# A hybrid decoder layer in split float32: 128-row score matmuls throughout, and FFN inputs that stream hi and lo of x side by side

## The chip, the core and the metric

The kernel runs on one core of a Trainium2 chip. TensorE (PE) multiplies matrices into PSUM, VectorE (DVE), ScalarE (ACT) and GpSimd (POOL) work on rows of 128 partitions, and SyncE (SP) issues most DMA transfers. The metric is the device time of one execution in microseconds, and less is better.

## What is computed

The layer works on 256 tokens of width 1024 in float32. Every sub-layer ends in x ← LayerNorm(2^0.25·x + sub-layer(x)).

```python
def swiglu_ffn(x, w_in, w_out):                       # 1024 -> 2 x 2816 -> 1024
    gate, up = jnp.split(x @ w_in, 2, axis=-1)
    return (jax.nn.silu(gate) * up) @ w_out

def dsa block(ql, qi, wi, t):                         # 128 queries, 16 heads
    logits = relu(einsum('bqhd,bsd->bqhs', qi, k_idx))          # index scores, d = 64
    score = where(causal, einsum('bqhs,bqh->bqs', logits, wi), -inf)
    _, idx = lax.top_k(score, 64)
    s = einsum('bqhr,bqkr->bqhk', ql, c_kv[idx]) - slopes * (t - idx)
    return softmax(where(idx <= t, s, -inf)) @ c_kv[idx]

x = LN(ALPHA * x + 0.5 * swiglu_ffn(x, ffn1))
h = x @ w_in                                          # gates, z, xbc, dt, q, c_kv, q_idx, k_idx, w_idx
y_ssd, y_att = ssd_branch(...), dsa_branch(...)       # Mamba-2 scan beside sparse attention
x = LN(ALPHA * x + (sigmoid(g_ssd) * (y_ssd @ w1) + sigmoid(g_att) * (y_att @ w2)) @ w_out)
x = LN(ALPHA * x + memory_xattn(x, mem))              # 4 heads of 256, 256 memory rows
x = LN(ALPHA * x + 0.5 * swiglu_ffn(x, ffn2))
```

## The kernel before

**Split products.** A float32 operand a is kept as two float32r tensors, hi (a rounded, made by an ACT copy) and lo = a − hi (a DVE subtraction); `split` makes both. A product takes three matmuls into one bank, hi·hi, hi·lo and lo·hi (`mm3`), and `mm` issues each. Tokens by features are kept transposed, as pairs of tiles `x0Th` and `x0Tl` ([128 features, 8 K blocks, 256 tokens]; `pairT` makes such a pair, x0T to x3T for the input and behind each norm).

**Weights** arrive by DMA in pieces of 128x1024 (`raw`, four buffers), and each is split at once into `whi` and `wlo` (six buffers of each, so three units of two pieces).

**FFN inputs.** `ffn_in` runs over 22 blocks of 128 features. One of them, a unit, needs a gate block and an up block, each 8 K blocks deep. `a_unit` puts both into one bank ([gate | up], 256 columns each) with 48 matmuls of 256 columns; then silu of the gate (ACT, L321), the product with up (DVE, L322) and a split into the features `ah` and `al`, which are the operands of the FFN's output (matmuls of 512 columns). In FFN 1 the first two units run K block by K block while weights and tokens arrive (`first_units`), in four banks; in FFN 2 the first three units run token block by token block (`by_token`) in another form.

**Mixers.** Three streams of work, sparse attention (`dsa`), the scan (`ssd`) and other projections (`fill_mixers`), are merged by `fly` into one order by a count of matmul work. A score group (`scores`, one head) is four matmuls: for each token block one with the queries' tile over all 128 partitions, and one over 64 partitions:

```python
self.mm(o, q[:, hh // 2, ts], kh, True, False)
self.mm(o, q[r, hh // 2, ts], kl[r], False, True)
```

The queries' tile `w2a` (even heads) or `w2e` (odd heads) holds hi on one half of the partitions and lo on the other (`project`); the keys `kh` hold hi on both halves, so one matmul over 128 rows gives hi·hi + lo·hi. The second one takes the half `r` with the queries' hi, and the keys' lo, for hi·lo. The index keys are `kidxh` and `kidxl`, those of the attention lie in a tile `kv` that `keys_values` makes four heads at a time (L763 to L766, with the values' hi and lo behind them in the same tile). The index scores are weighted and added up in `acc` on DVE, 64 keys are chosen there, and the attention's softmax runs on DVE and ACT.

**Banks and queues.** PSUM has four buffers `mm`, two `s` (scores) and two `t` (transposes). Each engine runs its instructions in the order that a scheduler has fixed.

Of the kernel before, what the change touches and what calls it, by code (L numbers as in the profile page):

```python
"""Hybrid decoder layer (macaron SwiGLU, Mamba-2 SSD beside DSA attention, memory
cross-attention, SwiGLU; DeepNorm post-LayerNorms) on one core.

float32 products go through the tensor engine as three float32r passes: every
operand a is split on the chip into hi (a rounded to float32r) and lo = a - hi,
and a.b = hi.hi + hi.lo + lo.hi accumulates in PSUM.  Small products stay float32.
"""
# [18 lines left out]
P = 128  # L26
# [24 lines left out]
class Layer:  # L51
# [28 lines left out]

    def tap(self, name, tile_):
        if name in self.taps:
            self.nc.sync.dma_start(self.taps[name], tile_)

# [4 lines left out]
    def weight(self, ap, piece=1024, pool=False):  # L89
        """loads, split into (hi, lo) in pieces of columns; pool: GpSimd makes the last lo."""  # L90
# [26 lines left out]
    def fly(self, *streams):  # L117
        """emits several streams of work in one order: a stream yields after a piece either
        how long (us of matmul work) its next piece should wait for the other engines, or the
        name of a result that another stream marks as done."""  # L120
# [17 lines left out]
    def mm3(self, out, a, b, start, stop):  # L138
        """out (+)= a^T b; a, b = (hi, lo)."""
        self.mm(out, a[0], b[0], start, False)  # L140
        self.mm(out, a[0], b[1], False, False)
        self.mm(out, a[1], b[0], False, stop)
# [5 lines left out]
    def a_block(self, ps, w, xT):  # L148
        """w: (hi, lo) [p, 128] per K block, stationary; ps [128 features, 256 tokens]."""
        for k, wk in enumerate(w):  # L150
            self.mm3(ps, wk, (xT[0][:, k, :], xT[1][:, k, :]), k == 0, k == len(w) - 1)

    def a_unit(self, ap, xT):
        """two 128-column blocks, [p, (2, kb, 128)], by 256 tokens in one bank."""
# [11 lines left out]
    def b_part(self, ps, w, xT, tb, k, start, stop):  # L166
        """tokens of block tb stationary, one K block w (hi, lo) [p, n] moving."""
# [11 lines left out]
    def b_chunk(self, wap, xT, evac, width=512):  # L179
        """[2, p, (4 kb, width)] columns, both token blocks in turn."""  # L180
# [32 lines left out]
    def constants(self):  # L213
# [7 lines left out]
        # attention keys: [0:256] for the queries of block 1, [256:384] for block 0  # L221
# [27 lines left out]
    def ln_params(self, i):  # L249
        """(scale, shift) of layer norm i, each as two halves of the columns."""  # L250
# [14 lines left out]
    def layer_norm(self, r, st, gb, dst):  # L265
        """r [128, 1024] with bn statistics st; dst may be r."""
# [11 lines left out]
    def res_evac(self, ps, c, r, x, scale, st):  # L278
        """r = scale * ps + x in the columns from c, with their statistics."""
# [11 lines left out]
    def ffn_in(self, win, xT, slots, first=None, by_token=0):  # L291
        """silu(gate) * up as hi/lo by features; the first by_token units run one token block
        after the other, so that the matmuls need not wait for the second."""
# [18 lines left out]
        for j in range(by_token, NFF):  # L312
            if first and j < 2:
                gate, up = first[2 * j:2 * j + 2]
            else:
                ps = self.a_unit(win[j], xT)
                gate, up = ps[:, :T], ps[:, T:]
            sg = self.small([P, T], "wa", bufs=4)
            if late:
                self.act_T(*late.pop())  # L320
            nc.scalar.activation(sg, gate, AF.Silu)  # L321
            nc.vector.tensor_mul(sg, up, sg)  # L322
# [6 lines left out]
    def first_units(self, xT):  # L329
        """tokens and the first two units of FFN 1 K block by K block, as they arrive; the  # L330
        tensor engine and the activation tables are warmed up meanwhile."""
# [9 lines left out]
        ps = [self.psum("mm")[:, :T] for _ in range(4)]  # L341
        for q in range(4):
# [10 lines left out]
            for k in range(2 * q, 2 * q + 2):  # L353
                for i in range(4):
                    c = slice((k % 2) * 512 + i * P, (k % 2) * 512 + (i + 1) * P)
                    self.mm3(ps[i], (hi[:, c], lo[:, c]), (xT[0][:, k, :], xT[1][:, k, :]), k == 0, k == KB - 1)
# [7 lines left out]
    def ffn_out(self, wout, act, finish, skew=3, last=False):  # L364
        """last: the columns that end last are finished in two parts."""
# [684 lines left out]
```

## Time and profile before

| | |
|---|---|
| Time of three runs | 835.6, 834.26, 835.91 us |
| Median | 835.6 us |
| Profiled execution, span | 833.3 us (no other time is recorded of it) |
| PE busy | 816.3 us, 98% of the span, 5726 matmuls |
| DVE, ACT, POOL busy | 560.8 us (67%), 424.1 us (51%), 68.1 us (8%) |
| Chain that ended last | PE 89%, DVE 4%, issue 4%, DMA 1%, ACT 1% |

The span runs from the first to the last instruction that the profile shows. An engine's busy share is an average over stages that differ. The granted clock is a fraction of TensorE's full speed: 1.00 is 2.4 GHz, 0.50 is 1.2 GHz. A timeline's line gives start, duration, engine, line, operation, tiles and count; durations of matmuls overlap, so what a matmul takes of PE's time is read from the starts. The stages lie as follows: FFN 1's input to about 135 us, its output to 195, the mixers to about 500, the cross-attention to about 635, FFN 2's input from there to 767 and its output to the end.

### The profile page before, as it was taken

The page shows a single profiled execution, that of the slowest core. Times are in us where ns is not written, and L with a number is a line of the kernel's source. Part 1 is how long each engine was busy: PE and PEld are TensorE (multiplying, and loading weights), DVE is VectorE, ACT ScalarE, POOL GpSimd, SP SyncE. Part 2 cuts the span into 40 slices and gives each one's busy share as a digit, 9 for nine tenths or more (in the row PEclk, how much of TensorE's full clock was granted, in tenths as well). Part 3 has the DMA queues.
Part 4 walks back from the last instruction along what each step waited for, and adds up shares of the span by engine and source line. Part 5 has one row for each costly group of instructions (what it writes and reads, how often), then busy time and mean ns, then how long its engine had stood idle before and what let it go on. Part 6 is the DMA issues. An engine that isn't in the chain of part 4 may idle for free.

```text
span 833.3 us, 14320 instructions
## 1 busy us (share of the span) xinstructions
PE 816.3 (98%) x5726; PEld 758.1 (91%) x5726; DVE 560.8 (67%) x870; ACT 424.1 (51%) x700; POOL 68.1 (8%) x69
## 2 busy tenths in 40 slices
PE   8999999999989899999999999999999999999996
PEld 7999999887889887899999998889988999999885
DVE  5665555449598988598778767965659755555445
ACT  5564444324666584477566545454444644444430
POOL 1100000000024351130000000100001000000000
PEclk9999999999999998999999999999999999999998
DMA  7886555554556513226444355685434755555531
GB/s 246 275 281 212 178 181 184 194 176 130 193 191 240 180 49 107 72 77 217 150 126 153 117 174 182 199 271 172 151 119 134 260 184 179 187 190 179 185 120 51
DMA packets 39923, 142.97 MB, mean 172 GB/s; under 512 B 4592, under 2 KB 4896, under 8 KB 39472
## 3 DMA queue, kind: packets, MB, share of 16 engines
q1 hardware_dynamic: 38016, 134.63, 49.0%
q0 software_dynamic: 1840, 7.43, 2.9%
q8 instruction: 45, 0.74, 0.4%
q14 instruction: 22, 0.18, 0.1%
HBM read 140.97 MB, written 1.06 MB: 170 GB/s over the span
## 4 chain that ended last, share of the span: by engine, by line
PE 89%; DVE 4%; issue 4%; DMA 1%; ACT 1%; POOL 0%; SPq 0%; DVEq 0%; ACTq 0%; POOLq 0%
PE ps_mm L111 79%; PE ps_s L111 5%; DVE wlo L146 2%; PE ps_t L115 2%; PE ps_t L111 2%; DMA raw<-in_ffn_in_dram 1%; DVE wa L430 1%; ACT whi L145 0%; DVE spp L503 0%; DVE bcT L430 0%; POOL rstd L262 0%; DVE bst L285 0%; ACT L432 0%; SPq L349 0%; DVE x L282 0%
## 5 line engine op out<-in xcount | busy, mean ns | idle before, releaser
L146 DVE TENSOR_TENSOR wlo<-raw,whi 128x1024 fp32r<-128x1024 f32 (+2 forms) x245 | 302.2, 1236 | 184.8 <-ACT whi L145 183.3
L145 ACT CAST whi<-raw 128x1024 fp32r<-128x1024 f32 (+2 forms) x253 | 262.4, 1041 | 222.1 <-PE ps_mm L111 111.5
L111 PE MATMUL ps_mm<-x1Th,whi 128*128 128x256 f32 x384 | 112.4, 293 | 0.0
L111 PE MATMUL ps_mm<-x1Tl,whi 128*128 128x256 f32 x384 | 110.9, 289 | 0.0
L111 PE MATMUL ps_mm<-x1Th,wlo 128*128 128x256 f32 x384 | 110.8, 289 | 0.0
L111 PE MATMUL ps_mm<-x0Th,whi 128*128 128x256 f32 x352 | 99.7, 285 | 1.4 <-ACT whi L145 1.3
L111 PE MATMUL ps_mm<-x0Tl,whi 128*128 128x256 f32 x352 | 99.2, 283 | 0.0
L111 PE MATMUL ps_mm<-x0Th,wlo 128*128 128x256 f32 x352 | 98.3, 284 | 0.7 <-DVE wlo L146 0.7
L111 PE MATMUL ps_mm<-x3Th,whi 128*128 128x256 f32 x304 | 86.2, 284 | 0.0
L111 PE MATMUL ps_mm<-x3Th,wlo 128*128 128x256 f32 x304 | 86.0, 283 | 0.0
L111 PE MATMUL ps_mm<-x3Tl,whi 128*128 128x256 f32 x304 | 86.0, 283 | 0.0
L111 PEld LDWEIGHTS ps_mm<-x1Th,whi 128*128 128x128 f32 x384 | 75.5, 197 | 1.3
L111 PEld LDWEIGHTS ps_mm<-x1Tl,whi 128*128 128x128 f32 x384 | 75.5, 197 | 0.4 <-issue 0.4
L111 PEld LDWEIGHTS ps_mm<-x1Th,wlo 128*128 128x128 f32 x384 | 75.7, 197 | 0.1
L111 PEld LDWEIGHTS ps_mm<-x0Th,whi 128*128 128x128 f32 x352 | 67.7, 192 | 2.5 <-ACT whi L145 2.5
L111 PEld LDWEIGHTS ps_mm<-x0Th,wlo 128*128 128x128 f32 x352 | 66.9, 192 | 1.3 <-DVE wlo L146 1.3
L111 PEld LDWEIGHTS ps_mm<-x0Tl,whi 128*128 128x128 f32 x352 | 67.7, 192 | 0.0
L111 PE MATMUL ps_mm<-whi,ah 128*128 128x512 f32 x154 | 60.4, 392 | 0.0
L111 PE MATMUL ps_mm<-wlo,ah 128*128 128x512 f32 x154 | 60.1, 390 | 0.0
L111 PE MATMUL ps_mm<-whi,al 128*128 128x512 f32 x154 | 59.9, 389 | 0.0
L111 PEld LDWEIGHTS ps_mm<-x3Tl,whi 128*128 128x128 f32 x304 | 58.4, 192 | 0.0
L111 PEld LDWEIGHTS ps_mm<-x3Th,wlo 128*128 128x128 f32 x304 | 58.4, 192 | 0.0
(305 smaller groups left out, 1708.9 us busy)
## 6 DMA issues: line engine op xcount, KB each, us to landing
raw<-in_ffn_in_dram SPq DMA_DIRECT2D x87, 512.0 KB, 4.4
raw<-in_ffn_out_dram SPq DMA_DIRECT2D x44, 512.0 KB, 4.4
raw<-in_w_xbc_dram SPq DMA_DIRECT2D x16, 512.0 KB, 4.3
raw<-in_w_gate_dram SPq DMA_DIRECT2D x16, 512.0 KB, 3.6
raw<-in_w_z_dram SPq DMA_DIRECT2D x8, 512.0 KB, 4.4
raw<-in_w_qidx_dram SPq DMA_DIRECT2D x8, 512.0 KB, 4.1
raw<-in_w_q_dram SPq DMA_DIRECT2D x8, 512.0 KB, 3.7
raw<-in_w_pssd_dram SPq DMA_DIRECT2D x8, 512.0 KB, 4.1
```

The lines of the kernel that those rows point to most:

```text
L111: self.nc.tensor.matmul(out, a, b, start=start, stop=stop)
L115: self.nc.tensor.transpose(out, in_, self.ident)
L145: self.nc.scalar.copy(hi, src)
L146: (engine or self.nc.vector).tensor_sub(lo, src, hi.bitcast(F32))
L430: self.last_conv = nc.vector.scalar_tensor_tensor(v[:, d:], src[:, :T - d], cw[:, 3 - d:4 - d], v[:, d:], op0=ALU.mult, op1=ALU.add)
```

## The change

In the FFN inputs hi and lo of x lie in one tile (`wideT`, [128, 2, 8, 256]). `pair` does a K block with two matmuls instead of three: the weights' hi past both halves (512 columns, into [hi·hi | hi·lo] of a whole bank) and the weights' lo past x hi (256 columns, onto the first half). `pair_unit` takes a bank for the gate and one for up. `join` adds the two halves: an ACT copy of the second into SBUF, and a DVE addition of the first. In `scores` the second matmul runs over 128 rows too, so that the lo halves of the queries meet the keys' lo as well; for this `keys_values` writes the keys' lo on both halves of the partitions (one more DVE subtraction per i, two per call, four calls), and the values' hi and lo move to a small tile of their own (`w2c`). Comments and docstrings are gone from the new file, which moves line numbers.

```diff
+    def wideT(self, name):
+        v = self.bp.tile([P, 2, KB, T], F32R, tag="g12", name=self.nm(name))
+        return v[:, 0], v[:, 1], v
+    def pair(self, ps, w, x, k):
+        self.mm(ps, w[0], x[2][:, :, k, :], k == 0, False)
+        self.mm(ps[:, :T], w[1], x[0][:, k, :], False, k == KB - 1)
+    def pair_unit(self, ap, xT):
+        out = []
+        for w in self.weight(ap):
+            ps = self.psum("mm")
+            for k in range(KB):
+                self.pair(ps, tuple(v[:, k * P:(k + 1) * P] for v in w), xT, k)
+            out.append(ps)
+        return out
+    def join(self, ps, out):
+        self.nc.scalar.copy(out, ps[:, T:])
+        self.nc.vector.tensor_add(out, out, ps[:, :T])
+        return out
...
-                ps = self.a_unit(win[j], xT)
-                gate, up = ps[:, :T], ps[:, T:]
-            sg = self.small([P, T], "wa", bufs=4)
+                gate, up = self.pair_unit(win[j], xT)
+            sg, u = self.small([P, T], "wa", bufs=4), self.small([P, T], "wa", bufs=4)
             if late:
                 self.act_T(*late.pop())
-            nc.scalar.activation(sg, gate, AF.Silu)
-            nc.vector.tensor_mul(sg, up, sg)
+            nc.scalar.activation(sg, self.join(gate, sg), AF.Silu)
+            nc.vector.tensor_mul(sg, self.join(up, u), sg)
...
-        ps = [self.psum("mm")[:, :T] for _ in range(4)]
+        ps = [self.psum("mm") for _ in range(4)]
...
-                    self.mm3(ps[i], (hi[:, c], lo[:, c]), (xT[0][:, k, :], xT[1][:, k, :]), k == 0, k == KB - 1)
+                    self.pair(ps[i], (hi[:, c], lo[:, c]), xT, k)
...
-            r, q = slice((hh % 2) * HD, (hh % 2 + 1) * HD), q[hh % 2]
+            q = q[hh % 2]
...
-                self.mm(o, q[r, hh // 2, ts], kl[r], False, True)
+                self.mm(o, q[:, hh // 2, ts], kl, False, True)
...
-        kl = s[:, 1024:1536].rearrange("p (a b) -> p a b", b=T)
-        vh, vl = s[:, 1536:1792], s[:, 1792:]
+        kl = s[:, 1024:].rearrange("p (i a b) -> p i a b", i=2, b=T)
+        v0 = self.small([P, 2, T], "w2c", F32R, 2)
+        vh, vl = v0[:, 0, :], v0[:, 1, :]
...
             nc.scalar.copy(kh[a, i], ps[a])
-            nc.vector.tensor_sub(kl[a], ps[a], kh[a, i].bitcast(F32))
             nc.scalar.copy(kh[b, i], ps[a])
+            nc.vector.tensor_sub(kl[a, i], ps[a], kh[a, i].bitcast(F32))
+            nc.vector.tensor_sub(kl[b, i], ps[a], kh[a, i].bitcast(F32))
...
-        xT = self.pairT(1, 2, "x0T")
+        xT = self.wideT("x0T")
```

(The last replacement stands four times, for x0T to x3T.)

**One unit of FFN 1 on PE.** Before, from the last K block of the gate into the first of up; each group of three stands eight times for each half, and the bank `ps_mm_806` is the same for both:

```order
L111 MATMUL ps_mm_806<-x0Th_72,whi_808 128x256
L111 MATMUL ps_mm_806<-x0Tl_73,whi_808 128x256
L111 MATMUL ps_mm_806<-x0Th_72,wlo_809 128x256
L111 MATMUL ps_mm_806<-x0Th_72,whi_814 128x256
L111 MATMUL ps_mm_806<-x0Tl_73,whi_814 128x256
L111 MATMUL ps_mm_806<-x0Th_72,wlo_815 128x256
```

After, the last K block of the gate, the first of up in another bank, and the first of the next unit in a third; each group of two stands eight times for each bank:

```order
L116 MATMUL ps_mm_715<-x0T_72,whi_704 128x512
L116 MATMUL ps_mm_715<-x0T_72,wlo_705 128x256
L116 MATMUL ps_mm_732<-x0T_72,whi_710 128x512
L116 MATMUL ps_mm_732<-x0T_72,wlo_711 128x256
...
L116 MATMUL ps_mm_771<-x0T_72,whi_760 128x512
L116 MATMUL ps_mm_771<-x0T_72,wlo_761 128x256
```

The 48 instructions of a unit have become 32, and a unit holds two banks instead of one.

**The same unit on DVE.** Before, the product of gate and up (`wa_867`), the features' lo (`al`), two subtractions for weights of a later unit, and the next unit's product:

```order
L322 TENSOR_TENSOR wa_867<-ps_mm_806,wa_867 128x256
L146 TENSOR_TENSOR al_264<-wa_867,ah_261 128x256
L146 TENSOR_TENSOR wlo_1073<-raw_1071,whi_1072 128x1024
L146 TENSOR_TENSOR wlo_1079<-raw_1077,whi_1078 128x1024
L322 TENSOR_TENSOR wa_933<-ps_mm_872,wa_933 128x256
```

After, the two additions of `join`, the product, a weight's lo, the features' lo and a weight's lo:

```order
L177 TENSOR_TENSOR wa_749<-wa_749,ps_mm_715 128x256
L177 TENSOR_TENSOR wa_750<-wa_750,ps_mm_732 128x256
L348 TENSOR_TENSOR wa_749<-wa_750,wa_749 128x256
L151 TENSOR_TENSOR wlo_879<-raw_877,whi_878 128x1024
L151 TENSOR_TENSOR al_231<-wa_749,ah_228 128x256
L151 TENSOR_TENSOR wlo_929<-raw_927,whi_928 128x1024
```

Two additions out of the banks now stand ahead of the product, which reads SBUF only.

**The end of the first two units on DVE.** Before, the last weights' lo of these units and of unit 2, and the two products, `wa_266` and `wa_271`:

```order
L146 TENSOR_TENSOR wlo_199<-raw_196,whi_198 128x1024
L146 TENSOR_TENSOR wlo_279<-raw_277,whi_278 128x1024
L146 TENSOR_TENSOR wlo_285<-raw_283,whi_284 128x1024
L322 TENSOR_TENSOR wa_266<-ps_mm_85,wa_266 128x256
L322 TENSOR_TENSOR wa_271<-ps_mm_87,wa_271 128x256
L146 TENSOR_TENSOR wlo_345<-raw_343,whi_344 128x1024
```

After, in the same place (`ps_mm_83` to `ps_mm_86` are the four banks of the two units):

```order
L151 TENSOR_TENSOR wlo_174<-raw_171,whi_173 128x1024
L151 TENSOR_TENSOR wlo_255<-raw_253,whi_254 128x1024
L151 TENSOR_TENSOR wlo_261<-raw_259,whi_260 128x1024
L177 TENSOR_TENSOR wa_233<-wa_233,ps_mm_83 128x256
L177 TENSOR_TENSOR wa_234<-wa_234,ps_mm_84 128x256
L177 TENSOR_TENSOR wa_243<-wa_243,ps_mm_85 128x256
L177 TENSOR_TENSOR wa_244<-wa_244,ps_mm_86 128x256
L348 TENSOR_TENSOR wa_233<-wa_234,wa_233 128x256
L151 TENSOR_TENSOR wlo_311<-raw_309,whi_310 128x1024
```

The same three subtractions come first; then the four additions, where only the two products stood.

**One call of keys_values on DVE.** Before, the keys' lo (L765, 64x512), the accumulation of index scores (`acc`) and the values' lo (L146) between the two subtractions:

```order
L765 TENSOR_TENSOR kv_3204<-ps_mm_3206,kv_3204 64x512
L669 SCALAR_TENSOR_TENSOR acc_3015<-wa_3230,widx_2227,acc_3015 128x256
L669 SCALAR_TENSOR_TENSOR acc_3015<-wa_3230,widx_2227,acc_3015 128x128
L146 TENSOR_TENSOR kv_3204<-ps_mm_3234,kv_3204 128x256
L669 SCALAR_TENSOR_TENSOR acc_3015<-wa_3255,widx_2227,acc_3015 128x256
L669 SCALAR_TENSOR_TENSOR acc_3015<-wa_3255,widx_2227,acc_3015 128x128
L765 TENSOR_TENSOR kv_3204<-ps_mm_3206,kv_3204 64x512
```

After, the keys' lo is written twice per i (L793 and L794), and the values' lo goes into `w2c`:

```order
L793 TENSOR_TENSOR kv_2980<-ps_mm_2983,kv_2980 64x512
L794 TENSOR_TENSOR kv_2980<-ps_mm_2983,kv_2980 64x512
L695 SCALAR_TENSOR_TENSOR acc_2791<-wa_3009,widx_2003,acc_2791 128x256
L695 SCALAR_TENSOR_TENSOR acc_2791<-wa_3009,widx_2003,acc_2791 128x128
L151 TENSOR_TENSOR w2c_2981<-ps_mm_3013,w2c_2981 128x256
L695 SCALAR_TENSOR_TENSOR acc_2791<-wa_3034,widx_2003,acc_2791 128x256
L695 SCALAR_TENSOR_TENSOR acc_2791<-wa_3034,widx_2003,acc_2791 128x128
L793 TENSOR_TENSOR kv_2980<-ps_mm_2983,kv_2980 64x512
L794 TENSOR_TENSOR kv_2980<-ps_mm_2983,kv_2980 64x512
```

The order around them is as it was. On PE the score groups stand where they stood, between the same neighbours.

## Rows read from the trace of the kernel before

**Rows 1.** The page: busy time by engine; granted clock in 40 slices, in tenths.
```profile
PE 816.3 (98%) x5726; PEld 758.1 (91%) x5726; DVE 560.8 (67%) x870; ACT 424.1 (51%) x700; POOL 68.1 (8%) x69
...
PEclk9999999999999998999999999999999999999998
```

**Rows 2.** The page: shares of the span of the chain that ended last, by line.
```profile
PE ps_mm L111 79%; PE ps_s L111 5%; DVE wlo L146 2%; PE ps_t L115 2%; PE ps_t L111 2%; DMA raw<-in_ffn_in_dram 1%; DVE wa L430 1%; ACT whi L145 0%; DVE spp L503 0%; DVE bcT L430 0%; POOL rstd L262 0%; DVE bst L285 0%; ACT L432 0%; SPq L349 0%; DVE x L282 0%
```

**Rows 3.** Windows of the FFNs: PE, PEld, DVE, ACT, POOL, clock, DMA share, GB/s.
```profile
60.00:130.00 70.00, 70.00 (x586) 70.00 (x585) 39.95 (x50) 33.13 (x50) 0.00 (x0) 1.00 0.58 193
690.00:755.00 65.00, 65.00 (x544) 65.00 (x543) 35.49 (x45) 30.81 (x46) 0.00 (x0) 1.00 0.54 181
```

**Rows 4.** Window of FFN 1's output, PE alone.
```profile
142.00:190.00 48.00, 48.00 (x214) 1.00 0.54 175
```

**Rows 5.** The chain of work in order of time, in FFN 2's output.
```profile
767.38 0.71 PE ps_t L111 x6
768.09 2.07 PE ps_mm L111 x9
```

**Rows 6.** Groups of instructions by line, form and tile.
```profile
L146 DVE TENSOR_TENSOR wlo<-raw,whi 128x1024 fp32r<-128x1024 f32 x239 | 297.3, 1246 | 181.2 <-ACT whi L145 179.7 <-PE ps_mm L111 0.5
...
L145 ACT CAST whi<-raw 128x1024 fp32r<-128x1024 f32 x247 | 258.1, 1049 | 218.9 <-PE ps_mm L111 111.2 <-issue 61.6 <-PE ps_t L111 24.2
...
L322 DVE TENSOR_TENSOR wa<-ps_mm,wa 128x256 f32<-128x256 f32 x41 | 17.0, 417 | 0.0
...
L321 ACT ACTIVATE wa<-ps_mm 128x256 f32<-128x256 f32 x41 | 15.6, 380 | 0.4 <-PE ps_mm L111 0.3
...
L765 DVE TENSOR_TENSOR kv<-ps_mm,kv 64x512 fp32r<-64x512 f32 x8 | 5.5, 688 | 0.4 <-ACT kv L764 0.2
```

**Rows 7.** Timelines of DVE and of PE at the end of the first two units.
```profile
16.90 3.73 DVE L146 TENSOR_TENSOR wlo<-raw,whi 128x1024 fp32r<-128x1024 f32 x3 [1.88 <-ACT whi L145]
...
18.18 0.62 PE L111 MATMUL ps_mm<-x0Th,wlo 128*128 128x256 f32 x3 [0.16 <-DVE wlo L146]
```

**Rows 8.** Timeline of PE at the first group of index scores.
```profile
297.46 0.28 PE L111 MATMUL ps_s<-kidxh,w2a 128*128 128x256 f32 x1
297.67 0.38 PE L111 MATMUL ps_s<-kidxl,w2a 64*128 64x256 f32 x1
297.98 0.38 PE L111 MATMUL ps_s<-kidxh,w2a 128*128 128x256 f32 x1
298.29 0.38 PE L111 MATMUL ps_s<-kidxl,w2a 64*128 64x256 f32 x1
298.61 0.66 PE L115 MATMUL ps_t<-ident,bcT 128*128 128x128 f32 x4
```

**Rows 9.** Timeline of PE at a group of attention scores.
```profile
423.72 1.30 PE L111 MATMUL ps_s<-kv,w2a 128*128 128x256 f32 x4
424.94 0.39 PE L111 MATMUL ps_mm<-yTh,whi 128*128 128x256 f32 x1
425.16 0.28 PE L111 MATMUL ps_mm<-yTl,whi 128*128 128x256 f32 x1
```

**Rows 10.** The chain of work at scores of the cross-attention.
```profile
571.80 1.42 PE ps_s L111 x12
```

**Rows 11.** Windows of index scores and top-k, and of the attention.
```profile
297.00:366.00 69.00, 69.00 (x435) 59.33 (x434) 55.32 (x119) 39.06 (x75) 18.43 (x10) 0.93 0.22 70
366.00:476.00 110.00, 110.00 (x824) 101.82 (x824) 88.57 (x190) 73.09 (x179) 5.58 (x5) 1.00 0.45 144
```

**Rows 12.** Windows of 1 us at two falls of the clock.
```profile
316.00:317.00 1.00, 1.00 (x4) 0.61 (x3) 0.97 (x2) 0.27 (x1) 0.00 (x0) 0.73 0.87 344
317.00:318.00 1.00, 1.00 (x3) 0.55 (x3) 0.97 (x4) 0.49 (x1) 0.00 (x0) 0.50 0.11 29
...
347.00:348.00 1.00, 1.00 (x3) 0.50 (x2) 1.00 (x3) 0.37 (x1) 0.98 (x1) 0.59 0.00 0
348.00:349.00 1.00, 1.00 (x5) 0.97 (x5) 0.93 (x1) 0.53 (x3) 0.44 (x1) 0.50 0.00 0
```

More of the change, by code (lines that the diff above doesn't have):

```diff
@@ L689, in softmax_in @@
             kv = self.kv[u]
-            ps = scores(qs[u], hh, kv[0][:, hh % 2, hh // 2, :], kv[1][:, hh // 2, :])
+            ps = scores(qs[u], hh, kv[0][:, hh % 2, hh // 2, :], kv[1][:, hh % 2, hh // 2, :])
             p = p_[h] = self.small([P, 384], "wa", bufs=4)
@@ L902, in run @@
             self.scale_res(x, tb)
-        xT = self.pairT(1, 2, "x1T")
+        xT = self.wideT("x1T")
         def fin(gb, dst, n=2):
@@ L943, in run @@
         gb = self.ln_params(2)
-        xT = self.pairT(1, 2, "x2T")
+        xT = self.wideT("x2T")
         self.proj_ln(t["w_out"], mT, x, gb, next_T(xT))
@@ L973, in run @@
         gb = self.ln_params(3)
-        xT = self.pairT(1, 2, "x3T")
+        xT = self.wideT("x3T")
         self.proj_ln(t["w_mo"], oT, x, gb, next_T(xT), (probs, turn, values))
```

## The prediction

> **What bounds the kernel now.** I read the page first: TensorE (PE) is busy 816.3 of 833.3 us and the chain that ended last runs over it for 89% of the span, 79% of that on the products into the mm banks, 5% on score matmuls [rows 1, 2]. So a shorter PE instruction stream shortens the kernel, as long as VectorE (DVE, 67% busy) and ScalarE (ACT, 51%) can follow. Shares over the whole span don't answer that, so each stage that the change touches is read by itself below.
>
> The profiled span is 833.3 us; the three runs have a median of 835.6, and I put the 2.3 us between them around the span, unchanged. Sums are made on the span, and a difference in the span is carried to the time. About 0.2%, 1.7 us, is what a measurement here can tell from no change.
>
> **FFN inputs.** For each 128-column block and K block there were three matmuls of 256 columns; now there is one of 512 and one of 256, the same 768 columns in two instructions. By the code, 39 units (20 in FFN 1, 19 in FFN 2) hold 16 such pairs, 624 pairs; the 32 pairs of the first two units wait for weights and are left out. In two stretches inside the FFNs PE has no idle time; 70.00 us hold 584 whole matmuls (586 less two cut at the edges) and 65.00 hold 542 [rows 3]: 0.1199 us for 256 columns, 5.76 us per unit of 48. In the FFN output, where all are 512 wide, 48.00 us hold 212: 0.2264 us [rows 4]. A pair would then save 3×0.1199−0.2264−0.1199 = 0.0134 us, 624 of them 8.4 us: the upper bound. The lower bound is from the one place where both widths take turns, FFN 2's output: six of 256 columns take 0.71 us and nine of 512 take 2.07, together 2.78 [rows 5], where 6×0.1199+9×0.2264 is 2.757. If the missing 0.023 us is the price of going from one width to the other and back, every pair pays it and loses 0.0096 us: 6.0 us more. The row can't say whether the surplus comes with each change of width or otherwise (the six also go to other banks than the nine), so I take most of the upper bound: **−5.6 us**, with −8.4 to +6.0 kept.
>
> The Trainium skill speaks against this part: "TensorE: Matmul & The Clock Gate", section "Back-to-back issue gap", has a fixed surplus of about 2.5 ns per matmul over its columns, by which 624 fewer instructions would save 1.6 us. Our two rows differ by 0.1065 us for 256 columns, so each matmul carries 0.0134 us beyond its columns here; the measured rows decide, and the sum goes by them.
>
> **Joins.** Each unit adds two ACT copies and two DVE additions of 128x256. Their nearest rows are the silu out of a bank, 380 ns, and the multiplication out of a bank, 417 ns [rows 6]. In the stretches of [rows 3] a unit (5.76 us) has 39.95/12.2 = 3.3 us of DVE and 33.13/12.2 = 2.7 us of ACT, so 4.1 and 3.5 after, below the 5.54 us that PE will need (16×0.3463). Following the order by hand (cast, copy, silu, copy, cast on ACT; weights' lo, two additions, multiplication, lo on DVE), with casts of 1049 and subtractions of 1246 ns [rows 6], the next unit's first addition comes about 7 us after this unit's gate bank ends, and that is inside the two units that four banks give. On ACT the copy of the up bank waits for PE's last matmul of the unit, and two casts of weights stand behind it; these are for a unit well ahead, so nobody waits for them yet. **0 us**, hidden behind PE; without that cover it is the last rival below. That hi and lo of x now share a tile, and that values' hi and lo moved, adds no instruction: 0.
>
> **The start.** Here a wait is new. All four banks are taken by the first two units, and unit 2's first matmul gets the first bank only after the DVE addition, which stands behind three weight subtractions. These start at 16.90 and end at 20.63 [rows 7]; before, the bank was free after a silu on ACT. PE ended the first two units near 20.2: the three lo matmuls from 18.18 on are followed by 14 more, (3+14)×0.12 after it [rows 7]. With the addition the bank is free at 20.63+0.42 = 21.05: **+0.9 us** (0 if subtractions come sooner, 1.7 if both additions must pass). Behind this wait on PE stands all of unit 2.
>
> **Score matmuls.** There are 32 groups (16 index heads, 16 attention heads), each of four matmuls of 256 columns: over 128 rows, 64, 128, 64. Starts in an index group are 297.46, .67, .98, 298.29, and the next instruction comes at 298.61 [rows 8]: 0.21+0.31+0.31+0.32 = 1.15 us, and a matmul behind a group takes 0.22 until the next instead of 0.12 (the first one behind the attention group: 424.94 to 425.16 [rows 9]). Together 1.25 where four at full pace take 0.48: **0.77 saved**. The attention group runs from 423.72 to 425.16, the matmul after it included: 1.44−5×0.12 = 0.84. That 128 rows are the cure is shown by the cross-attention's scores, same shapes over 128 rows: twelve in 1.42 us, 0.118 each [rows 10]. The lowest count, only what lies inside a group (1.15−0.48 = 0.67), gives 21.4 us, the highest (0.84) 26.9. I take **−24.6 us**. What it costs: keys' lo on both partition halves, 8 more DVE subtractions of 64x512 at 688 ns [rows 6], counted below.
>
> **Clock.** The granted clock is 1.00 almost everywhere [rows 1], but 0.93 in 297 to 366 [rows 11]. In 1 us slices it falls from 316 and from 347 on and is 0.50 (1.2 GHz) a microsecond later; 4 and 3 matmuls begin in the microsecond of the fall, as in the score groups, where at full pace there are 8 [rows 12]. 69.00×0.07 = 4.8 us is lost there. If those pauses go, it should mostly come back; new waits could bring it down again. **−4.0 us** (0 to −4.8).
>
> **DVE in the mixers: the price of all this.** From 297 to 366 DVE is busy 55.32 us of 69.00, from 366 to 476 88.57 of 110.00 [rows 11]; PE has no idle time there, so PE sets the pace. After the change PE needs 69.00−16×0.77−4.0 = 52.7 and 110.00−12.3 = 97.7; DVE, with four of the added subtractions in each (0.69 apiece), 58.1 and 91.3. In the first stretch DVE is then the longer by 5.4 us, and in the second it has 6% left. The order on PE hardly changes, so PE, and all that stands behind on it, waits for what DVE is late with: converted queries, the accumulation of index scores ahead of top-k, weights' lo. Lower bound 0 (DVE's lag is absorbed by weights three units ahead and made up before 500), upper bound: DVE keeps half of its idle time of the first stretch (13.7/2) on top of 5.4, 12.3. I take the 5.4 and some of the second stretch: **+7 us**.
>
> **Sum.** −5.6+0.9−24.6−4.0+7 = −26.3: span 807.0, time **809.3 us**.
>
> **Rivals.**
> *DVE takes over in the mixers.* It loses 13 to 19 instead of 7, because its operations wait for ACT and PE in turn. For it: its work comes to 110% and 93% of PE's in the two stretches, and two engines that wait for each other at such shares seldom reach the longer one's sum. Against: weights can be prepared ahead, and most of the second stretch's 6% is free. 815 to 821.
> *DVE hides it all.* −8.4+0.5−24.6−4.8 = −37.3: 798.3. For it: weights are prepared three units ahead; against: top-k runs on DVE between index scores and attention, and nothing is ahead of it.
> *The widths cost.* What a pair saves goes with the turn from 512 to 256 columns and back. With half of the surplus of [rows 5] a pair keeps 0.0134−0.0115 = 0.0019 us, 1.2 in all: 813.7. With all of it the FFN loses 6.0: 820.9. For it: that row; against: it shows the surplus once in fifteen matmuls, along with a change of banks. "TensorE: Matmul & The Clock Gate" of the Trainium skill, by its gap alone, would put the time at 813.3.
> *The pauses are not from the 64 rows* but from the alternation of banks or operands; then scores gain nothing, DVE is no bound and the clock stays: −5.6+0.9: 830.9. Against it stands [rows 10].
> *Slower.* ACT and DVE wait for each other in each FFN unit (copy, silu, addition, multiplication, cast, lo are one chain over two in-order engines), and this cycle becomes the pace of 39 units. Strictly in turn they need 4.1+3.5 = 7.6 us. All other terms give −20.7, so it decides from (20.7+1.7)/39 = 0.57 us above 5.76, at 6.3 us per unit; at 7.6 the FFNs lose 72 and the time is 887. Against it: the casts and subtractions of weights, 4.6 us of the 7.6, depend on DMA alone.
>
> **Chances.** Forecast (DVE term 0 to 12, FFN gaining) 0.47; DVE takes over 0.20; all hidden 0.14; widths cost 0.10; pauses stay 0.05; slower 0.04. The range 798 to 822 holds the first four cases, with a little of their edges outside, and leaves out the last two. The first five are all faster by over 1.7 us; 0.02 is kept for a mixture that ends near no change: faster 0.94, within 0.2% 0.02, slower 0.04.
>
> **What would show it.** Score groups with starts 0.12 us apart; units of 32 matmuls in 5.54 us inside the FFNs without idle time on PE (5.9 if widths cost, over 6.3 if the joins bound); a granted clock of 1.00 from 297 on; a PE wait of near 0.9 us for the first addition at about 20; and in the mixers PE waits for DVE of some 7 us in sum, most ahead of the attention. The forecast is wrong if those waits pass 20 us, or if PE waits for a join anywhere but at the start.

## The result and the profile after

The changed kernel takes 815.08 us in the median of four runs (813.47 to 816.25), beside 835.75 for the kernel before on the same chip: a ratio of 0.9757, 95% interval 0.9735 to 0.9778. It is faster by 2.4%. The forecast was 809.3, in a range of 798 to 822.

The page of the changed kernel, span 812.9 us: busy time by engine, the granted clock in tenths, and the two lines of the chain that ended last.

```profile
PE 789.4 (97%) x5070; PEld 717.5 (88%) x5070; DVE 592.4 (73%) x960; ACT 448.4 (55%) x782; POOL 68.2 (8%) x69
...
PEclk9999999999999999799999999999999999999999
...
PE 74%; DVE 11%; issue 8%; ACT 4%; DMA 2%; POOL 1%; SPq 0%; DVEq 0%; ACTq 0%; POOLq 0%
PE ps_mm L116 69%; DVE wlo L151 3%; PE ps_t L116 2%; PE ps_t L120 2%; DMA raw<-in_ffn_in_dram 2%; ACT whi L150 1%; PE ps_s L116 1%; DVE acc L695 1%; DVE acc L702 1%; DVE wa L456 1%; DVE m L701 1%; DMA raw<-in_w_pssd_dram 0%; POOL rstd L289 0%; DVE kv L794 0%; DVE kv L793 0%
```

PE is still busy 97% of a span that is 20.4 us shorter, but its share of the chain has fallen from 89% to 74% and DVE's has risen to 11% [rows 1, 2]. One slice of the clock now shows 7. It lies where the index scores are. By the first starts of the matmuls on each tile, the 20.4 us come from these stretches:

| stretch (from the end of the one above) | before | after | difference |
|---|---|---|---|
| to FFN 1's output | 135.5 | 134.3 | −1.2 |
| to the first index scores | 162.0 | 159.7 | −2.3 |
| to the first attention scores | 69.4 | 64.8 | −4.6 |
| to the projection of the attention's output | 118.8 | 110.5 | −8.3 |
| to FFN 2's output | 281.5 | 277.5 | −4.0 |
| to the end | 66.1 | 66.1 | 0.0 |

Nothing of the change runs in the second stretch; over all kernels of this study it takes 159.7 to 164.1 us. PE's pauses in its last 70 us sum to 4.4 to 6.7 us, and in all but three of the kernels the clock falls there. A difference of 2 us between two profiles is therefore not read as an effect here.

What PE waits for in the changed kernel up to 500 us, the eight largest (sum, times, longest):

```profile
PE ps_t L120 <- DVE cTl L501: 3.1, 1, 3.1
PE ps_s L116 <- ACT wa L692: 2.6, 1, 2.6
PE ps_mm L116 <- ACT whi L150: 2.1, 4, 1.0
PE ps_t L116 <- DVE warm L362: 1.3, 1, 1.3
PE ps_s L116 <- DVE w2a L668: 1.2, 1, 1.2
PE ps_mm L116 <- ACT S0xe L613: 1.0, 1, 1.0
PE ps_mm L116 <- DVE wa L177: 0.9, 1, 0.9
PE ps_t L120 <- DVE yTl L231: 0.9, 1, 0.9
```

New among them are the wait for the join at the start (`wa` L177, 0.9) and four in the mixers: for a relu of the index scores (`wa` L692), for a state of the scan (`S0xe`), for converted queries (`w2a`) and for the lo of the scan's output (`yTl`). The windows of the mixers (PE, PEld, DVE, ACT, POOL, clock, DMA share, GB/s), which answer to [rows 11], and of the two FFNs, which answer to [rows 3]:

```profile
294.00:358.80 64.80, 59.99 (x438) 58.71 (x437) 56.20 (x120) 37.20 (x75) 19.34 (x10) 0.89 0.22 74
358.80:469.30 110.50, 108.24 (x897) 107.02 (x898) 96.33 (x203) 77.30 (x186) 4.67 (x5) 1.00 0.47 158
...
60.00:130.00 70.00, 70.00 (x398) 60.68 (x397) 51.79 (x80) 44.29 (x80) 0.00 (x0) 1.00 0.61 201
660.00:740.00 80.00, 80.00 (x463) 70.55 (x462) 57.13 (x87) 48.01 (x88) 0.00 (x0) 1.00 0.58 192
```

In the index stretch PE now stands still for 64.80−59.99 = 4.8 us, where it never did (the waits for `wa` L692, `S0xe` and `w2a`, the last of them just ahead of the first attention scores), and the clock is 0.89 instead of 0.93. In the FFNs it never stops: no join is waited for there. Less the two matmuls at the edges, a pair takes 70.00/198 = 0.3535 us in FFN 1 and 80.00/230.5 = 0.3471 in FFN 2, against 3×0.1199 = 0.3597 before.

The scores themselves, the timeline of PE at one group of index scores:

```profile
297.63 0.28 PE L116 MATMUL ps_mm<-cTh,wlo 128*128 128x256 f32 x1
297.75 0.28 PE L116 MATMUL ps_s<-kidxh,w2a 128*128 128x256 f32 x1
297.87 0.27 PE L116 MATMUL ps_s<-kidxl,w2a 128*128 128x256 f32 x1
297.98 0.28 PE L116 MATMUL ps_s<-kidxh,w2a 128*128 128x256 f32 x1
```

and at a group of attention scores:

```profile
407.57 0.72 PE L116 MATMUL ps_s<-kv,w2e 128*128 128x256 f32 x4
408.12 0.28 PE L116 MATMUL ps_mm<-yTh,whi 128*128 128x256 f32 x1
408.24 0.28 PE L116 MATMUL ps_mm<-yTl,whi 128*128 128x256 f32 x1
```

Starts in the first are 0.11 to 0.12 us apart, where they were 0.21 to 0.32 [rows 8]. The Trainium skill, "TensorEngine Tiling (Array Packing)", section "Key Properties", says that a change of the tiling mode drains TensorE. The rows agree with that as far as they go: starts 0.31 us apart where 64 and 128 rows take turns [rows 8], 0.11 to 0.12 where all have 128.

### The profile page after: what moved, and what is told of

Read it like the earlier page. It is cut to its first block, busy times and chain, and to the rows that moved or that the text cites. A ratio compares the mean times of both kernels' runs of the same rounds, so it can differ in the third digit from the quotient of the medians.

```text
span 812.9 us, 13145 instructions
## 1 busy us (share of the span) xinstructions
PE 789.4 (97%) x5070; PEld 717.5 (88%) x5070; DVE 592.4 (73%) x960; ACT 448.4 (55%) x782; POOL 68.2 (8%) x69
## 4 chain that ended last, share of the span: by engine, by line
PE 74%; DVE 11%; issue 8%; ACT 4%; DMA 2%; POOL 1%; SPq 0%; DVEq 0%; ACTq 0%; POOLq 0%
PE ps_mm L116 69%; DVE wlo L151 3%; PE ps_t L116 2%; PE ps_t L120 2%; DMA raw<-in_ffn_in_dram 2%; ACT whi L150 1%; PE ps_s L116 1%; DVE acc L695 1%; DVE acc L702 1%; DVE wa L456 1%; DVE m L701 1%; DMA raw<-in_w_pssd_dram 0%; POOL rstd L289 0%; DVE kv L794 0%; DVE kv L793 0%
## 5 line engine op out<-in xcount | busy, mean ns | idle before, releaser
L116 PE MATMUL ps_mm<-x1T,whi 128*128 128x256 f32 x768 | 143.9, 288 | 0.0
L116 PE MATMUL ps_mm<-x0T,whi 128*128 128x512 f32 x352 | 123.7, 400 | 2.9 <-ACT whi L150 2.1
L116 PEld LDWEIGHTS ps_mm<-x1T,whi 128*128 128x128 f32 x768 | 122.3, 195 | 0.0
L116 PE MATMUL ps_mm<-x1T,wlo 128*128 128x256 f32 x384 | 110.2, 287 | 0.0
L116 PE MATMUL ps_mm<-x3T,whi 128*128 128x512 f32 x304 | 105.6, 392 | 0.0
L116 PE MATMUL ps_mm<-x0T,wlo 128*128 128x256 f32 x352 | 97.0, 282 | 0.3 <-DVE wlo L151 0.3
L116 PE MATMUL ps_mm<-x3T,wlo 128*128 128x256 f32 x304 | 85.1, 280 | 0.0
L116 PEld LDWEIGHTS ps_mm<-x0T,whi 128*128 128x128 f32 x352 | 65.8, 188 | 20.6 <-ACT whi L150 3.6
L116 PEld LDWEIGHTS ps_mm<-x1T,wlo 128*128 128x128 f32 x384 | 75.1, 195 | 0.0
L116 PEld LDWEIGHTS ps_mm<-x3T,whi 128*128 128x128 f32 x304 | 56.9, 187 | 12.4
L116 PEld LDWEIGHTS ps_mm<-x0T,wlo 128*128 128x128 f32 x352 | 65.7, 189 | 1.6 <-DVE wlo L151 1.4
L116 PE MATMUL ps_mm<-whi,al 128*128 128x512 f32 x154 | 59.9, 389 | 0.0
L177 DVE TENSOR_TENSOR wa<-wa,ps_mm 128x256 f32<-128x256 f32 x82 | 34.0, 418 | 30.2 <-ACT wa L176 30.1
```

The costliest lines, as they stand in the source:

```text
L116: self.nc.tensor.matmul(out, a, b, start=start, stop=stop)
L177: self.nc.vector.tensor_add(out, out, ps[:, :T])
```

## The experiments

All are compared with the kernel before on the same chip. Its median was 835.28 us beside `e1` to `e4`, 835.66 beside `e5` to `e8`, 836.29 beside `e9`, `e12` and `e13`, and 835.42 beside `e15`.

**One part at a time.** `e1_scores` is the kernel before with the 128-row scores and the doubled keys' lo alone; `e2_ffn` has the FFN inputs alone.

The line that parts them, as `e1_scores` changes it in the kernel before; `keys_values` goes with it, and `e2_ffn` is the changed kernel with both put back:

```diff
-                self.mm(o, q[r, hh // 2, ts], kl[r], False, True)
+                self.mm(o, q[:, hh // 2, ts], kl, False, True)
```

> Only the 128-row scores, with the keys' lo on both halves; the FFN inputs are as before. Theory A (the changed kernel's mixers lost their gain to waits for ACT and DVE and to a lower clock, and the FFN has no part in it): the mixers become as long as in the changed kernel, so the time is 835.7 - 13 = about 822.5 us, with PE pauses of 4 to 7 us and a granted clock near 0.9 in the index scores. Rival (the mixers only became short of DVE because the FFN's joins left it behind): PE pauses under 2 us, clock 1.00, time 811 to 815.

> Only the FFN inputs with 512-column passes and joins; the scores are as before. Theory A (a matmul costs its columns plus a fixed 0.0134 us, and the joins are hidden): FFN 2 gives 4.0, FFN 1 4.2 less what its longer 512-column matmuls take, less 0.9 at the start: 828 to 830 us. Rival (turning from 512 to 256 columns costs, in FFN 1 at least, and what the changed kernel gained was in the scores): 833 to 836.

Measured: 821.44 us (ratio 0.9812, 0.9775 to 0.9849) and 829.68 (0.9932, 0.9916 to 0.9949). The parts give 13.8 and 5.6 us, together 19.4 of the 20.7 that both give: they add up, as far as the first one's interval, 6 us wide, can tell. With the scores alone the mixers look as in the changed kernel:

```profile
299.40:364.20 64.80, 59.96 (x439) 58.70 (x437) 56.20 (x120) 37.27 (x75) 19.34 (x10) 0.89 0.22 74
364.20:474.80 110.60, 108.22 (x897) 106.97 (x898) 96.26 (x203) 77.22 (x186) 4.64 (x5) 1.00 0.47 158
```

Same pauses, same clock, to 0.1 us. So the joins of the FFN have no part in the mixers' waits: theory A holds, for `e2_ffn` too.

**The price of a matmul.** `e3_ffn_three` keeps banks and joins, but cuts the 512-column matmul in two, for 7 of 8 K blocks.

```diff
-        self.mm(ps, w[0], x[2][:, :, k, :], k == 0, False)
+        if k == 0:
+            self.mm(ps, w[0], x[2][:, :, k, :], True, False)
+        else:
+            self.mm(ps[:, :T], w[0], x[0][:, k, :], False, False)
+            self.mm(ps[:, T:], w[0], x[1][:, k, :], False, False)
```

> The changed kernel, but in each 128-column block the K blocks 1 to 7 stream x hi and x lo in two matmuls of 256 columns instead of one of 512; joins and two banks a unit stay. Against the changed kernel this adds 39 x 14 = 546 matmuls and no columns. Theory A (fixed 0.0134 us a matmul): 546 x 0.0134 = 7.3 us more than the changed kernel, some 822 us, and units of 5.73 us in both FFNs. Rival 1 (long 512-column matmuls in FFN 1 are what holds its gain down): only 5 us more there and in FFN 2 together, since FFN 1 loses its surplus: 820. Rival 2 (a fixed cost of some 2.5 ns): 816.5.

Measured: 822.15 us (0.9847, 0.9824 to 0.9871), 7.1 more than the changed kernel, as theory A said. The windows inside FFN 1 and FFN 2 (PE, clock, DMA share, GB/s) put it otherwise:

```profile
60.00:130.00 70.00, 70.00 (x563) 1.00 0.61 197
660.00:740.00 80.00, 80.00 (x643) 1.00 0.56 184
```

Less two at the edges, a unit of 46 matmuls takes 5.74 us in both, where 16 pairs of the changed kernel take 5.66 in FFN 1 and 5.55 in FFN 2. That is 0.006 us for each added matmul in FFN 1 and 0.013 in FFN 2, together 5.2 us, near the 5 of rival 1: in FFN 1 the cut also takes away what the 512-column matmuls lose there. The other 1.9 us of the time are not found in these windows, and the interval of the time is too wide to part the two. Out is rival 2: no column was added, and in FFN 2 a matmul carries a fixed price of 0.013 us. By "TensorE: Matmul & The Clock Gate" of the Trainium skill, section "Back-to-back issue gap", it would be about 2.5 ns; this run does not agree.

**Casts first.** In `keys_values` the third ACT cast waits for two DVE subtractions; here all casts come first.

```diff
             nc.scalar.copy(kh[b, i], ps[a])
+        for i in range(2):
+            a, b = slice(i * HD, (i + 1) * HD), slice((1 - i) * HD, (2 - i) * HD)
             nc.vector.tensor_sub(kl[a, i], ps[a], kh[a, i].bitcast(F32))
```

> The changed kernel with one reordering: keys_values issues its four ACT casts first and its four DVE subtractions after them, so that the third cast no longer waits for the first two subtractions. Theory A (ACT stood 3.4 us at that cast, behind it the relus of the index scores, PE paused 2.6 us for their banks, and the clock fell to 0.5 after the pause): that pause goes and most of the 7 us lost to the clock in this stretch with it: 806 to 812 us. Rival (DVE's amount of work sets the index stretch, whoever waits for whom): within 1.5 us of the changed kernel, 813.5 to 816.5, with the same PE pauses in other places.

Measured: 820.76 us (0.9822, 0.9803 to 0.984): no gain, and 5.7 more than the changed kernel. PE's waits in the index stretch were these:

```profile
PE ps_mm L116 <- ACT S0xe L613: 3.8, 1, 3.8
PE ps_s L116 <- DVE w2e L668: 0.4, 1, 0.4
PE ps_mm L116 <- DVE wlo L151: 0.2, 1, 0.2
```

The pause of 2.6 us at the scores' bank is gone, as expected; the one at the scan's state grew from 1.0 to 3.8. The stretch took 64.9 us. Theory A fell here: the handoff was real, but taking it away moved the wait to another operation. The rival's time is missed too. Of the profile's 6.5 us over the changed kernel's, 4.4 lie ahead of the index scores (71.4 us instead of 67.0 from the first x projection by features, with the clock at 0.93 instead of 0.97) and 1.4 in FFN 1, both in code that this edit does not touch. Why all four runs of this build are that long (818.9 to 821.4) stays open.

**Less work for DVE.** `e5_lo_by_act` copies the second half of the keys' lo by ACT, `e8_norm_act` divides in the softmax on ACT, `e9_lo_norm` does both.

The first edit, then the second:

```diff
-            nc.vector.tensor_sub(kl[b, i], ps[a], kh[a, i].bitcast(F32))
+            nc.scalar.copy(kl[b, i], kl[a, i].bitcast(F32))
...
-                nc.vector.tensor_scalar_mul(p[:, s], p[:, s], sm[:, tb:tb + 1])
+                nc.scalar.activation(p[:, s], p[:, s], AF.Copy, scale=sm[:, tb:tb + 1])
```

> The changed kernel, but the second half of the keys' lo is copied by ACT from the first instead of subtracted once more by DVE (8 DVE subtractions of 0.69 us less, 8 ACT copies more). Theory B (DVE's amount of work sets the index stretch; casts first only moved the pause to another place): of 4.8 us of PE pauses between the first index scores and the first attention scores some 2 to 3 go, with some of the clock: 810 to 813.5 us. Rival (the queue on ACT sets it, where the relus of the index scores stand behind other work): pauses as long or longer, 815 to 819.

> The changed kernel, but the softmax's division by the sum (two DVE multiplications a head, 16 heads) is done on ACT. DVE loses some 8 us of work in the attention, ACT gains as much. Theory B (DVE at 96 of 110 us is what PE waits for there): the 2.3 us of PE pauses in the attention go, and a little of what is lost in longer matmul gaps: 811.5 to 813.5 us. Rival (in the attention the waits are single handoffs, not an amount): within 1 us of the changed kernel.

> The changed kernel with both moves from DVE to ACT: the second half of the keys' lo as a copy, and the softmax's division. DVE loses 14 us of work in the mixers, ACT gains 13. Theory B: both stretches are PE's then, 58 to 60 and 107 to 109 us: 806 to 810. Theory C (single pauses and the clock behind them count, not the sum): the pauses behind ACT's queue stay at 4 us before the index scores' banks and 3 us at the start of the attention, 811 to 815.

Measured: 815.87 (0.9753, 0.9712 to 0.9795), 814.34 (0.9737, 0.9685 to 0.9788) and 817.14 us (0.9756, 0.9693 to 0.9818). None is clear of the changed kernel: `e5_lo_by_act` and `e8_norm_act` come out, in time, where their rivals stood, `e9_lo_norm` above both theories. The windows of `e9_lo_norm`:

```profile
298.30:358.70 60.40, 56.06 (x439) 55.27 (x437) 53.46 (x118) 38.24 (x77) 21.14 (x10) 0.94 0.23 79
358.70:472.30 113.60, 109.02 (x897) 107.10 (x898) 87.55 (x165) 91.23 (x224) 4.63 (x5) 1.00 0.46 154
```

DVE has 141.0 us of work in the two instead of 152.5. The index stretch is 4.4 us shorter, but the attention is 3.1 us longer, though DVE has 26 us to spare in it: PE stands 3.1 us there for DVE's lo of the scan's output (`yTl`), once. Theory B, that the amount of DVE's work sets the pace, does not carry the time. In the index stretch alone it may have a part: `e5_lo_by_act` too is 4.8 us shorter there (60.0 us), and 3.5 longer in the attention.

**128 rows in the index scores only.**

```diff
-            ps = scores(qs[u], hh, kv[0][:, hh % 2, hh // 2, :], kv[1][:, hh % 2, hh // 2, :])
+            ps = scores(qs[u], hh, kv[0][:, hh % 2, hh // 2, :], kv[1][:, hh // 2, :], True)
```

The added argument keeps the lo matmul on 64 rows; `keys_values` is as before.

> The changed kernel with 128 rows only in the index scores; the attention's lo matmuls run over 64 rows as before, and keys_values is as before (no added subtraction). Theory B: the attention takes again what it took before, 118.8 us from its first scores to the last x projection, 8.3 more; the index stretch is a little shorter than in the changed kernel, as DVE has 2.8 us less in it: together 820 to 823 us. Rival (the added subtractions cost nothing, PE waits for the index scores' own ACT and DVE work): index stretch as in the changed kernel, 64.8 us, with the same pauses: 823 to 824.5.

Measured: 828.61 us (0.991, 0.988 to 0.9939), over 4 us more than either theory said. Its windows:

```profile
295.50:359.10 63.60, 56.75 (x438) 55.37 (x437) 55.56 (x118) 37.04 (x75) 17.75 (x10) 0.95 0.23 75
359.10:483.50 124.40, 121.99 (x896) 113.28 (x897) 96.13 (x197) 77.76 (x186) 4.66 (x5) 0.97 0.44 140
```

The index stretch took 63.6 us with 6.8 us of pauses, without any added subtraction: so these waits are not the price of the doubled keys' lo. The attention took 124.4 us, 5.6 more than in the kernel before, with a pause of 2.4 us for `yTl` and a clock of 0.97, which loses 124.4×0.03 = 3.7 us.

**Heads further apart, two ways.** `e7_spread` delays each index head; `e12_interleave` puts a block of the projection (24 matmuls) behind each pair of heads.

First the delay, then the pairs:

```diff
-                yield 0.3
+                yield 1.0
...
         yield from project("w_qidx", 0, 1.0)
+        yield from project("w_qidx", 1, 1.0)
         for u in range(4):
-            if u < 3:
-                yield from project("w_qidx", u + 1, 1.0)
-            else:
+            if u == 3:
                 yield 3.0
+            nxt = project("w_qidx", u + 2, 1.0) if u < 2 else iter(())
...
                 yield 0.3
+                if hh % 2:
+                    for r in nxt:
+                        yield r
+                        break
+            yield from nxt
```

> The changed kernel, with the next index head due 1.0 instead of 0.3 us of matmul work after the last, which puts more other matmuls between the heads of the last two of the four units, and the attention some 90 matmuls later. Theory B: a shift of work between stretches that leaves DVE's amount as it is; pauses in the index stretch fall by what moves behind it, but come back before the attention: 813 to 817 us. Rival (the heads follow each other too closely for two banks of scores, and that alone makes the pauses): pauses in the index stretch under 2 us and the clock at 1.00 there: 806 to 811.

> The changed kernel with the index heads in another place: the projection of the unit after next goes between the pairs of heads of a unit (24 matmuls each), where so far four heads of a unit follow one another. No work is added or taken away on any engine. Theory C (the index stretch has 52 us of work for PE; the rest is single pauses of 2.6 us and more, made by heads that come faster than ACT and DVE can empty two banks, and the lower clock that follows them): the pause at the scores' bank goes, the stretch falls from 64.8 to 55 to 60 us: 805 to 811. Theory B (DVE's amount of work, 56 us in the stretch, sets it): the pauses move to the attention's first scores, stretch 63 to 65 us: 814 to 816.

Measured: 821.16 us (0.9821, 0.9779 to 0.9862) and 809.39 (0.9661, 0.9597 to 0.9726). The delay made a new pause of 4.1 us for the keys (`kv` L794) and a clock of 0.88; its time is above both theories. The pairs are the best version of this study, 27 us below the kernel before; their interval lies just below the changed kernel's. The windows of `e12_interleave`:

```profile
296.40:357.90 61.50, 57.27 (x438) 55.80 (x437) 57.55 (x122) 37.81 (x76) 18.40 (x10) 0.94 0.24 78
357.90:466.80 108.90, 107.92 (x899) 106.95 (x898) 95.56 (x201) 76.97 (x185) 4.65 (x5) 1.00 0.49 160
```

What PE waits for in the first of them:

```profile
PE ps_s L116 <- ACT wa L692: 3.8, 3, 1.8
PE ps_mm L116 <- DVE w2e L668: 0.3, 1, 0.3
PE ps_mm L116 <- DVE wlo L151: 0.2, 1, 0.2
```

DVE's work is as before the edit (57.55 and 95.56 instead of 56.20 and 96.33). An order alone shortened the two stretches, by 3.3 and 1.6 us; in this profile the untouched stretch ahead of them is 2.5 us longer. The time is in theory C's range, its mechanism only in part: the pause at the scores' bank did not go but became three, 3.8 us in sum, the longest 1.8, and all pauses fell only from 4.8 to 4.2 us. What came back is the clock, 0.94 instead of 0.89, and the stretch is 1.5 us longer than the 55 to 60 expected.

**Both orders, and the pairs with the softmax on ACT.**

> The heads in pairs between the projection's blocks, and the four casts of keys_values ahead of its four subtractions. With the pairs alone ACT stood 4.0 us at a cast of the keys behind DVE's subtractions, and PE then 1.75 us at a bank of the scores, in the first half of the index scores. Theory C: this pause goes, and as it is a short one little of the clock comes with it: index stretch 58 to 61 us, 805 to 809. Rival (as casts first alone showed, the wait only moves on to the next operation of ACT's queue): 809 to 813.

> The heads in pairs as in the other kernel of this call, and the softmax's division on ACT. Theory C: index stretch 55 to 60, attention 108 to 109.5 us: 803 to 809. Theory B: 811 to 815.

Measured: 810.35 us (0.9715, 0.9689 to 0.9741) and 809.95 (0.9664, 0.9592 to 0.9737): neither is clear of the pairs alone, and the second lies between its two theories. PE's waits in the index stretch of `e15_interleave_casts`:

```profile
PE ps_mm L116 <- DVE w2e L668: 3.7, 1, 3.7
PE ps_s L116 <- ACT wa L692: 0.9, 1, 0.9
```

The pause at the scores' bank went down to 0.9 us, and one of 3.7 at a conversion of queries (`w2e` L668) came in its place: the rival's reading, as with the casts alone. The stretch, 59.9 us, is all the same as short as theory C had it.

**The clock behind a pause.** One more reading, from the traces at hand: windows of PE, of 2 and of 10 us (busy, count, clock, DMA share, GB/s), in the changed kernel, ahead of and behind two of its pauses,

```profile
308.00:310.00 2.00, 0.00 (x0) 1.00 0.01 4
310.00:312.00 2.00, 1.44 (x12) 1.00 0.00 0
312.00:314.00 2.00, 2.00 (x13) 0.53 0.29 68
314.00:316.00 2.00, 2.00 (x13) 0.61 0.51 195
...
324.00:326.00 2.00, 0.98 (x8) 0.94 0.78 236
326.00:336.00 10.00, 10.00 (x45) 0.50 0.41 147
```

and with the heads in pairs (`e12_interleave`), where the scan's matmuls of 64 columns, which fill 326 to 333 above, run in 326 to 334:

```profile
326.00:328.00 2.00, 2.00 (x19) 1.00 0.75 248
328.00:330.00 2.00, 1.72 (x16) 1.00 0.97 301
330.00:332.00 2.00, 2.00 (x16) 1.00 0.48 188
...
341.00:343.00 2.00, 0.26 (x3) 1.00 0.76 176
343.00:345.00 2.00, 1.98 (x11) 0.65 1.01 406
345.00:347.00 2.00, 2.00 (x11) 0.50 0.56 213
```

In these places PE is paused at full clock, and the half clock (1.2 GHz) comes up to two microseconds later, when it works again. The same scan matmuls run at 1.00 where only a pause of 0.3 us precedes them, and at 0.50 for 10 us where one of 1.0 does. Not every pause is paid for so: the two around 358 in the changed kernel (1.2 and 0.9 us) leave the clock at 1.00. In all 14 traces, between 100 and 790 us, there are 59 pauses of PE of 1.0 to 4.1 us; at 32 of them the clock falls to 0.50, within the pause or up to 2 us behind it, and at 27 it does not, some of 2.5 to 3.3 us among them. That a pause causes the fall is therefore argued and not shown; no run filled a pause with other matmuls.

What the two cost can be told apart. In the index stretch of the changed kernel and ten others (all experiments but `e2_ffn` and `e7_spread`) PE's pauses sum to 4.2 to 6.9 us, and the time at 1.2 GHz goes from 3.4 us (`e13_interleave_norm`, `e15_interleave_casts`) over 6.8 and 10.2 to 13.7 (changed kernel, `e1_scores`, `e4_casts_first`). Less the pauses and half of that time, 52.3 to 54.2 us are left in every one of them. So the versions differ there mostly by their clock, and with nearly the same pauses (2.6, 1.0 and 1.2 us; 2.6, 1.2 and 1.2) the changed kernel has 13.7 us of it and `e8_norm_act` 10.2.

## Why the prediction came out as it did

The direction, the range and most terms held; the time is 5.8 us above the forecast. What failed is the clock term. Point by point:

- *FFN inputs*, −5.6: right in kind. FFN 2 gave 4.0 us, in its window 0.0126 a pair, where the upper bound was 0.0134. FFN 1 gave 2.1 (1.2 and the 0.9 lost at the start), half as much, since a pair takes 0.3535 there. Together −6.1, though the stretch to FFN 1's output differs by up to 2.4 us between kernels with the same FFN 1 (134.2 to 136.6). The rival that the turn of widths costs is out in FFN 2, which turns as often and pays next to nothing; in FFN 1 a pair loses 0.0072 of the 0.0134 us, and why is open.
- *Joins*, 0: held, in both FFNs of the changed kernel. In `e4_casts_first`, `e9_lo_norm` and `e13_interleave_norm` PE waited for a join near 53 and 56 us too, 0.4 to 1.2 us in sum.
- *The start*, +0.9: held. PE waited 0.85 us for the first addition, until 21.19.
- *Score matmuls*, −24.6: held in the rows. In the attention a group with the matmul behind it takes 408.24−407.57 = 0.67 us, where it took 1.44 [rows 9]; the 16 groups together are 12.4 us shorter, where 12.3 were expected.
- *DVE in the mixers*, +7: PE's pauses there are 4.8 and 2.3, together 7.1, and were put at 5.4 and 1.6. The size was right; the reason was not. It was to be the sum of DVE's work; the run with 11.5 us less of it (`e9_lo_norm`) gained nothing, and the one with the same sum in another order (`e12_interleave`) gained 5.7. It is single waits behind ACT's and DVE's queues, three in the index stretch and six in the attention.
- *Clock*, −4.0: the term that failed. It was said that the loss of 4.8 us should mostly come back when the pauses inside the scores go. It did not: the stretch ran 10.2 us at 1.2 GHz before (316.5 to 323.3 and 347.2 to 350.6), which loses 5.1 (4.8 by the rounded 0.93), and 13.7 us after (312.1 to 315.5 and 325.8 to 336.0), which loses 6.8. Both falls after come behind new pauses, of 2.6 and 1.0 us; that these take the place of the many short ones is the reading at hand, not shown. From −4.0 to +1.7 makes 5.7 us, nearly the whole error.

With the measured sizes the sum is −6.1+0.9−24.6+7.1+1.7 = −21.0, beside −20.4 of the span. That it closes so well is in part luck: 2.3 us of the span come from a stretch that the change does not touch, and the mixers kept 2.9 us more than the sum has, 1.7 of them in the attention (−12.3+2.3 = −10.0 by the sum, −8.3 seen). There a wait takes more than the idle time that the profile lists, since durations of matmuls overlap:

```profile
361.53 0.40 PE L116 MATMUL ps_mm<-x1T,whi 128*128 128x256 f32 x2
362.78 0.66 PE L120 MATMUL ps_t<-ident,xtok 128*128 128x128 f32 x4 [0.85 <-DVE yTl L231]
```

The second matmul of the first line starts at 361.65, so the next one comes 1.13 us behind it instead of 0.12 for a wait of 0.85. Compared one by one with the kernel before, the starts in the attention are 12.6 us closer, nearly all at the scores, and at 17 other places 4.2 us further apart, with 2.2 us of idle time listed.

## What to carry to other kernels

When an engine at 98% got a shorter stream here, part of the gain turned into waits at single handoffs of the engines behind it, and removing one handoff twice handed the wait to another (`e4_casts_first`, `e15_interleave_casts`): compare the sum of pauses by stretch, not the one wait that is gone. Another order of the score groups (the pairs) was worth more in the whole time than moving 11.5 us of work between engines, and most of what it gave in its stretch came by the clock. Add up the clock apart from the pauses, from the trace after the change, and do not book it as a gain before.

## What the runs showed of the hardware

- A float32r matmul of 256 or 512 columns costs 0.013 us beyond its columns (0.1199 and 0.2264 us at full clock [rows 3, 4]; 0.013 for each matmul that `e3_ffn_three` adds in FFN 2, 0.006 in FFN 1).
- A pair of a 512- and a 256-column matmul takes 0.3535 us in FFN 1 and 0.3471 in FFN 2, both at full clock. By the starts the difference lies behind the wide one: 0.236 us to the next start in FFN 1, 0.230 in FFN 2. With seven of eight wide ones cut in two, both FFNs run at the same pace (561 and 641 whole matmuls in 70 and 80 us). What slows the wide ones in FFN 1 is open.
- Four score matmuls that alternate between 128 and 64 rows take 0.77 us longer, with the matmul behind them, than four of 128 rows (1.44 and 0.67 us in the attention).
- At 32 of 59 pauses of PE of 1.0 to 4.1 us the granted clock went down to 1.2 GHz, for 3.4 to 20.5 us; at 27 it did not.
